# Attention scores of a 512-token hybrid block: one float32 product with half-zero keys per head, or two fp32r products of stacked query parts

## Chip, cores and metric

The kernel runs on one core of a Trainium2 chip. The metric is the device time of one execution in microseconds (us); less is better. The program is straight-line: five in-order instruction queues (TensorE, VectorE, ScalarE, GpSimd, and SyncE, which issues the DMAs), tied by semaphores.

## What is computed

Two transformer-like blocks run one after the other on 512 tokens of width 1024. The change lies in the first block's sliding-window attention. It has 16 query heads and 4 key/value heads of 64 features, 16 "meta" tokens that every query sees, and a window of 128 tokens:

```python
q = (q * (HEAD_DIM ** -0.5)).reshape(b, l, N_KV_HEADS, Q_PER_KV, HEAD_DIM)
...
keys = jnp.concatenate([k_meta, kn], axis=1)       # 16 meta + 2 blocks of 128
sc = jnp.einsum('bqkgd,bskd->bkgqs', qn, keys).astype(jnp.float32)
mask = jnp.concatenate([meta_ok, valid], axis=1)
p = sink_softmax(sc, mask, sink)
return jnp.einsum('bkgqs,bskd->bqkgd', p.astype(vals.dtype), vals)
```

The queries, keys and values come from `hn @ w_in`, where `hn` is a normalised state: each token's row carries a factor `r`, its reciprocal root mean square. Beside the attention the block has a state-space part (`s5_ssm`) and gates, all from the same `w_in`. Feed-forward layers and the second block make up the rest of the run.

## The kernel before

**Projections.** All big products are made of fp32r matmuls on split operands: a weight tile `raw` is fetched by DMA, ScalarE copies it to `whi` (fp32r), VectorE writes the rest `raw - whi` to `wlo` (`sub`, line 66), and `mm3` (line 182) adds three products hi*hi, lo*hi, hi*lo for each of eight slices of 128. A projection of 512 columns is 24 matmuls into one PSUM bank. `nat` (line 198) does the same for the values with 256 columns.

**The attention stage** (about 420 to 640 us of the run). After the state-space inputs `u` come two key projections. Each result is multiplied by `R` (the factor `r` spread over the columns) into `kf` and copied by ScalarE and GpSimd into window tiles `kw`: for each of two key heads a tile of 128 partitions whose other 64 partitions hold zeros, with three windows of 272 columns (16 meta columns and two blocks). Then the value projection, and four of eight query projections; `query` multiplies each by 0.125 and `R` on VectorE (line 83). One query tile holds two heads, one per 64 partitions.

Then a loop over eight units (two key pairs `pp` times four token blocks `n`). Unit `ui` issues:

- `scores1`: for each of four query tiles and both key heads `s_` one float32 product of 128 queries with W keys (144 columns for `n` = 0, "short", else 272, "long"; line 734). The zeros of `kw` take out the head that isn't meant. VectorE reads each product from PSUM in one instruction that adds the mask and finds the row maximum (line 737, called the reduction below), and later adds the sink terms; ScalarE takes the exponentials.
- in units 0, 1, 3 and 5 `ssm_quarter`: tiles `U`, `M`, `G`, `bstl`, `tab` come by DMA into single buffers; products with `bstl` (line 576) in two halves; VectorE multiplies and adds into `sq` tiles; two scans (lines 586, 587); more `sq` products; then per quarter 12 products (lines 597 to 599), a gelu, and a write to DRAM. The next quarter's `U` and `M` can be fetched only when the last of these 12 is done.
- in units 0 to 3 one more `query`; later three gate projections, which serve as work for TensorE.
- `turn1` and `values1` of the unit before: transposes (lines 766, 776) and products with the values (788, 792).

PSUM has two banks for projections and the state-space part (`b`), three for scores (`q`), two for transposes (`t`), one for the output (`o`).

**Order.** The recording layer schedules instructions within a queue, so that TensorE's and VectorE's queues interleave units, quarters and projections. Each queue then runs strictly in its order: an instruction that waits holds all behind it.

Of the kernel before, what the change touches and what calls it, by code (L numbers as in the profile page):

```python
# [53 lines left out]
def body(nc, tc, A, out, es):  # L54
# [13 lines left out]
    def mul(o, a, b, e=None):  # L68
        return tt(o, a, b, ALU.mult, e)
# [15 lines left out]
    def act(o, a, f, **kw):  # L85
        return SC.activation(o, a, f, **kw)  # L86
# [115 lines left out]
    def v2(t):  # L202
        return t.rearrange("p (a n) -> p a n", a=2)
# [453 lines left out]
    with tc.tile_pool(name="m1", bufs=1) as mp:  # L657
        att = mp.tile([P, 8, S], F32, name="att")
        with tc.tile_pool(name="m2", bufs=1) as ap_:
            kz = [[ap_.tile([P, 3, 272], F32, name=f"kw{mo}{e}") for e in range(2)] for mo in range(2)]  # L660
            for gs in kz:
                for e, g in enumerate(gs):
                    GP.memset(g[64 - 64 * e:128 - 64 * e], 0.0)
# [7 lines left out]
            kw = []  # L671
            for mo in range(2):
                p = proj(wload("w_in", 1024), P, 0, z, C528)
                f = ap_.tile([P, T1], F32, name="kf", tag=f"sq{mo}")
                mul(v2(f), p[:, :, :264], v2(R))

                gs = kz[mo]
                for e, g in enumerate(gs):
# [26 lines left out]
            qf = []  # L705

            def query():
# [5 lines left out]
            for _ in range(4):  # L713
                query()
# [8 lines left out]
            def scores1(u):  # L723
# [60 lines left out]
            def values1(u):  # L784
# [9 lines left out]
                act(att[:, pp * 4:pp * 4 + 4, n * P:(n + 1) * P], po.rearrange("p (i q) -> p i q", i=4), AF.Copy)  # L794

            units = [(pp, n) for pp in range(2) for n in range(4)]
            for ui in range(len(units) + 1):
# [4 lines left out]
                if ui < 4:  # L802
                    query()
                elif 5 <= ui < 8:
                    gate(zp.tile([P, aw], F32, name="acc" if ui == 5 else "sq", bufs=1 if ui == 5 else 2)[:, :S])
                elif ui == 8:
                    with tc.issue_after(last["sc"].ins):
                        for i in range(2):
                            gate(mp.tile([P, S], F32, name=f"q{i}"))
# [5 lines left out]
        with tc.tile_pool(name="m3", bufs=2) as gp_:  # L815
# [13 lines left out]
            for i in range(8):  # L829
# [3 lines left out]
                stt(ga, ga, 1.0, att[:, i], ALU.add, ALU.mult)  # L833
# [758 lines left out]
```

## Time and profile before

| | us |
|---|---|
| runs (3): lowest, median, highest | 2589.45, 2594.76, 2596.42 |
| profiled execution, whole | 2593.17 |
| its span, first to last instruction | 2591.3 |
| TensorE busy in the span | 2566.1 |
| VectorE busy in the span | 1573.6 |
| ScalarE busy in the span | 995.3 |

The profiled execution is 1.9 us longer than its span. A matmul's end is modelled in these profiles, so matmuls that follow each other are priced by the distance of their starts. A float32 matmul shows as two records.

### The profile page before, as it was taken

The page shows a single profiled execution, that of the slowest core. Times are in us where ns is not written, and L with a number is a line of the kernel's source. Part 1 is how long each engine was busy: PE and PEld are TensorE (multiplying, and loading weights), DVE is VectorE, ACT ScalarE, POOL GpSimd, SP SyncE. Part 2 cuts the span into 40 slices and gives each one's busy share as a digit, 9 for nine tenths or more (in the row PEclk, how much of TensorE's full clock was granted, in tenths as well). Part 3 has the DMA queues.
Part 4 walks back from the last instruction along what each step waited for, and adds up shares of the span by engine and source line. Part 5 has one row for each costly group of instructions (what it writes and reads, how often), then busy time and mean ns, then how long its engine had stood idle before and what let it go on. Part 6 is the DMA issues. An engine that isn't in the chain of part 4 may idle for free.

```text
span 2591.3 us, 35009 instructions
## 1 busy us (share of the span) xinstructions
PE 2566.1 (99%) x13918; PEld 2188.1 (84%) x13918; DVE 1573.6 (61%) x2859; ACT 995.3 (38%) x1562; POOL 84.9 (3%) x98
## 2 busy tenths in 40 slices
PE   9999999999999999999999999999999999999999
PEld 8999999766888888888888878888878888888887
DVE  7985445685467544467665775555763457655566
ACT  5222223445343222245544454333353234433333
POOL 0000001000000000000000001000000010100000
PEclk9999999999999999999999999999999999999999
DMA  5443324332333333322111223333232222333331
GB/s 182 132 136 113 92 90 133 104 94 68 100 97 101 98 98 96 95 90 70 53 58 62 76 78 108 98 98 98 82 100 58 75 65 83 120 98 98 98 96 67
DMA packets 87749, 243.32 MB, mean 94 GB/s; under 512 B 20081, under 2 KB 26097, under 8 KB 87458
## 3 DMA queue, kind: packets, MB, share of 16 engines
q1 hardware_dynamic: 87586, 241.08, 30.2%
q8 instruction: 110, 1.80, 0.3%
q14 instruction: 53, 0.43, 0.1%
HBM read 229.11 MB, written 11.93 MB: 93 GB/s over the span
## 4 chain that ended last, share of the span: by engine, by line
PE 96%; DVE 2%; issue 0%; SPq 0%; ACT 0%; DMA 0%; DVEq 0%
PE ps_b L182 27%; PE ps_q L182 19%; PE ps_t L182 18%; PE mm L182 16%; PE ps_b L198 5%; PE ps_o L1258 1%; PE ps_q L1230 1%; PE ps_o L792 1%; PE ps_q L734 1%; PE ps_t L1246 1%; PE ps_q L1384 1%; DVE sq L66 1%; PE ps_b L1457 0%; PE ps_t L198 0%; PE ps_t L776 0%
## 5 line engine op out<-in xcount | busy, mean ns | idle before, releaser
L86 ACT ACTIVATE whi<-raw 128x1024 fp32r<-128x1024 f32 (+2 forms) x418 | 432.8, 1038 | 1001.3 <-PE ps_b L182 297.5
L66 DVE TENSOR_TENSOR wlo<-raw,whi 128x1024 fp32r<-128x1024 f32 (+2 forms) x418 | 502.0, 1203 | 331.5 <-ACT whi L86 329.6
L182 PE MATMUL ps_b<-zh,whi 128*128 128x512 f32 (+1 forms) x692 | 272.8, 394 | 2.9 <-DVE sq L66 0.9
L182 PE MATMUL ps_b<-zl,whi 128*128 128x512 f32 (+1 forms) x692 | 269.8, 390 | 0.0
L182 PE MATMUL ps_b<-zh,wlo 128*128 128x512 f32 (+1 forms) x692 | 269.6, 390 | 0.0
L182 PE MATMUL ps_q<-zh,whi 128*128 128x512 f32 (+1 forms) x488 | 189.3, 388 | 1.2 <-ACT zh L86 1.2
L182 PE MATMUL ps_q<-zl,whi 128*128 128x512 f32 (+1 forms) x488 | 189.4, 388 | 0.0
L182 PE MATMUL ps_q<-zh,wlo 128*128 128x512 f32 (+1 forms) x488 | 189.2, 388 | 0.0
L182 PE MATMUL ps_t<-zh,whi 128*128 128x512 f32 x476 | 185.6, 390 | 0.6 <-ACT zh L86 0.6
L182 PE MATMUL ps_t<-zl,whi 128*128 128x512 f32 x476 | 185.6, 390 | 0.0
L182 PE MATMUL ps_t<-zh,wlo 128*128 128x512 f32 x476 | 185.2, 389 | 0.0
L182 PE MATMUL mm<-zh,whi 128*128 128x264 f32 x800 | 162.4, 284 | 5.8 <-ACT whi L86 5.8
L182 PE MATMUL mm<-zl,whi 128*128 128x264 f32 x800 | 161.8, 284 | 0.1
L182 PE MATMUL mm<-zh,wlo 128*128 128x264 f32 x800 | 161.3, 283 | 0.0
L182 PEld LDWEIGHTS ps_b<-zh,whi 128*128 128x128 f32 (+1 forms) x692 | 129.2, 187 | 33.6 <-issue 2.8
L182 PEld LDWEIGHTS ps_b<-zl,whi 128*128 128x128 f32 (+1 forms) x692 | 129.3, 187 | 28.8 <-issue 2.3
L182 PEld LDWEIGHTS ps_b<-zh,wlo 128*128 128x128 f32 (+1 forms) x692 | 129.2, 187 | 28.5 <-issue 1.1
L182 PEld LDWEIGHTS mm<-zh,whi 128*128 128x128 f32 x800 | 124.2, 189 | 5.8 <-ACT whi L86 5.8
L182 PEld LDWEIGHTS mm<-zl,whi 128*128 128x128 f32 x800 | 124.0, 189 | 0.4 <-DVE zl L83 0.4
L182 PEld LDWEIGHTS mm<-zh,wlo 128*128 128x128 f32 x800 | 123.9, 189 | 0.0
L182 PEld LDWEIGHTS ps_q<-zh,whi 128*128 128x128 f32 x488 | 91.6, 188 | 20.8 <-ACT zh L86 2.1
L182 PEld LDWEIGHTS ps_q<-zl,whi 128*128 128x128 f32 x488 | 91.6, 188 | 20.4 <-DVE zl L66 1.3
(586 smaller groups left out, 5340.2 us busy)
## 6 DMA issues: line engine op xcount, KB each, us to landing
raw<-in_ffn_w_dram SPq DMA_DIRECT2D x130, 512.0 KB, 3.5
raw<-in_w_up_dram SPq DMA_DIRECT2D x88, 512.0 KB, 3.7
raw<-in_w_down_dram SPq DMA_DIRECT2D x44, 512.0 KB, 3.6
raw<-in_w_in_dram SPq DMA_DIRECT2D x32, 512.0 KB, 3.6
raw<-in_mla_o_dram SPq DMA_DIRECT2D x16, 512.0 KB, 3.6
raw<-in_ple_g_dram SPq DMA_DIRECT2D x16, 512.0 KB, 3.7
raw<-in_glu_dram SPq DMA_DIRECT2D x8, 512.0 KB, 3.6
raw<-in_w_out_dram SPq DMA_DIRECT2D x8, 512.0 KB, 3.4
```

The lines of the kernel that those rows point to most:

```text
L66: return (e or V).tensor_tensor(o, a, b, op=op)
L86: return SC.activation(o, a, f, **kw)
L182: last["pe"] = PE.matmul(o[:, i, :c1 - c0], lhs, x[k][r][:, c0:c1], start=(k == 0 and j == 0), stop=(k == kt - 1 and j == 2))
L198: PE.matmul(o[:m, :n], x[k][a][:, t0:t0 + m], w[b][:, kk_ * c + m0:kk_ * c + m0 + n], start=(k == 0 and i == 0), stop=(k == kt - 1 and i = ...
L734: last["sc"] = PE.matmul(pq[s_][:, :W], qf[pp * 4 + i][:, n * P:(n + 1) * P], kw[pp][s_][:, max(n - 1, 0), :W])
L792: PE.matmul(po[64 * s_:64 * s_ + 64], vb[n - 1 + j][:, kv * 64:kv * 64 + 64], pT[s_][:, j], start=False, stop=(j == 1))
L1230: PE.matmul(p[:, :N], d["q"][e][:, bs], d["k"][e][:, :N], start=False, stop=True)
L1246: PE.transpose(pt[:, kt * P:(kt + 1) * P], sc[:, kt * P:(kt + 1) * P], ident)
L1258: PE.matmul(po[:, b * P:(b + 1) * P], vt[:, kt, e * P:(e + 1) * P], pT[:, kt * P:(kt + 1) * P], start=(kt == 0), stop=(kt == b))
L1384: PE.matmul(pu[c][:, :256], ek[b][rows, hc], vt[hh][rows, b])
```

## The change

For each unit the four query tiles are split once: ScalarE copies 64 partitions of all four (`x`, 64x512) to one half of a tile `qs` in fp32r, and VectorE writes the rest `x - copy` to the other half. The keys are split likewise (`keys`): `kh` holds the fp32r copy of the keys twice, on both halves of the partitions, and `kl` their rest twice. One product of `qs` with `kh` and one with `kl`, added in PSUM, then stand for the float32 product. The short windows are computed 256 columns wide, and read 144 wide.

The factor `r` of the queries is now applied by the reduction, which takes it as a value per partition (`r[:, n:n + 1]` instead of 1.0). So `query` is a plain scaled copy, on ScalarE. `keys(0)` follows the key projections; `keys(1)` is made in unit 3 into the same buffers. The second `kf` lies in the tile `acc`. The result `att` is two tiles, and the last two gates share a tile `gt`; both take over query buffers.

```diff
-            kz = [[ap_.tile([P, 3, 272], F32, name=f"kw{mo}{e}") for e in range(2)] for mo in range(2)]
...
-                f = ap_.tile([P, T1], F32, name="kf", tag=f"sq{mo}")
+                f = zp.tile([P, aw], F32, name="acc") if mo else ap_.tile([P, T1], F32, name="kf", tag="sq0")
                 mul(v2(f), p[:, :, :264], v2(R))
-
-                gs = kz[mo]
-                for e, g in enumerate(gs):
-                    r_ = slice(64 * e, 64 * e + 64)
-                    cpy = (lambda o, i: act(o, i, AF.Copy)) if e else GP.tensor_copy
-                    cpy(g[r_, 0], f[r_, :272])
-                    GP.tensor_copy(g[r_, 1:, 0:NM], f[r_, 0:NM].unsqueeze(1).to_broadcast([64, 2, NM]))
-                    for n in range(1, 3):
-                        cpy(g[r_, n, NM:], f[r_, NM + n * P:NM + (n + 2) * P])
-                kw.append(gs)
+                kf.append(f)
+
+            def keys(pp):
+
+                out_ = []
+                for e in range(2):
+                    a = slice(64 * e, 64 * e + 64)
+                    f = kf[pp][a]
+                    kh, kl = (ap_.tile([P, 3, 272], F32R, name=f"k{n}{e}") for n in "hl")
+                    for o in (a, slice(64 - 64 * e, 128 - 64 * e)):
+                        for w_, c in ((0, f[:, :272]), *((n, f[:, NM + n * P:NM + (n + 2) * P]) for n in (1, 2))):
+                            t = slice(NM if w_ else 0, 272)
+                            act(kh[o, w_, t], c, AF.Copy)
+                            sub(kl[o, w_, t], c, kh[a, w_, t].bitcast(F32))
+                        for k in (kh, kl):
+                            GP.tensor_copy(k[o, 1:, :NM], k[o, 0:1, :NM].to_broadcast([64, 2, NM]))
+                    out_.append((kh, kl))
+                return out_
+
+            kw = {0: keys(0)}
...
                 p = proj(wload("w_in", 1024), P, 0, z, C512)
-                t = (mp if len(qf) < 2 else ap_).tile([P, S], F32, name=f"q{len(qf)}")
-                stt(t, p[:, 0, :], 0.125, Rr, ALU.mult, ALU.mult)
-                qf.append(t)
...
+                act(qf[i // 4][:, i % 4], p[:, 0], AF.Copy, scale=0.125)
...
+                qs = []
+                for s_ in range(2):
+                    t = ap_.tile([P, 4, P], F32R, name=f"qs{s_}", bufs=2)
+                    a, o = slice(64 * s_, 64 * s_ + 64), slice(64 - 64 * s_, 128 - 64 * s_)
+                    x = qf[pp][a, :, n * P:(n + 1) * P]
+                    act(t[a], x, AF.Copy)
+                    sub(t[o], x, t[a].bitcast(F32))
+                    qs.append(t)
                 for i in range(4):
                     pq = [pss("q"), pss("q")]
                     for s_ in range(2):
-                        last["sc"] = PE.matmul(pq[s_][:, :W], qf[pp * 4 + i][:, n * P:(n + 1) * P],
-                                               kw[pp][s_][:, max(n - 1, 0), :W])
+                        for k in range(2):
+                            last["sc"] = PE.matmul(pq[s_][:, :max(W, 256)], qs[s_][:, i],
+                                                   kw[pp][s_][k][:, max(n - 1, 0), :max(W, 256)],
+                                                   start=(k == 0), stop=(k == 1))
                     for s_ in range(2):
-                        V.tensor_tensor_reduce(sc[s_][:, i, :W], pq[s_][:, :W], mk, 1.0, -3.0e38,
+                        V.tensor_tensor_reduce(sc[s_][:, i, :W], pq[s_][:, :W], mk, r[:, n:n + 1], -3.0e38,
                                                ALU.add, ALU.max, st[s_][0][:, i:i + 1])
...
+                    query(4 + ui)
+                if ui == 3:
+                    kw[1] = keys(1)
```

Three places of the new order matter below. The first is VectorE's queue from the fourth query to the first reductions. Before (`q_5392` is the fourth query, `sq_...` quarter 0's products, `ISA sc,at` a reduction):

```order
L83 SCALAR_TENSOR_TENSOR q_5392<-ps_b,R 128x512
L737 ISA sc,at_5398<-ps_q,mask 128x144
L737 ISA at_5398 128x1
L737 ISA sc,at_5401<-ps_q,mask 128x144
L737 ISA at_5401 128x1
L737 ISA sc,at_5398<-ps_q,mask 128x144
L737 ISA at_5398 128x1
L66 TENSOR_TENSOR wlo<-raw,whi 128x1024
```

Now:

```order
L66 TENSOR_TENSOR sq_5507<-ps_b,tab 128x264
L66 TENSOR_TENSOR sq_5510<-ps_b,tab 128x264
L66 TENSOR_TENSOR wlo<-raw,whi 128x1024
L66 TENSOR_TENSOR sq_5508<-ps_b,tab 128x264
L66 TENSOR_TENSOR qs_5414<-q_5274,qs_5414 64x512
L66 TENSOR_TENSOR sq_5509<-ps_b,tab 128x264
L66 TENSOR_TENSOR sq_5507<-ps_b,tab 128x264
L66 TENSOR_TENSOR sq_5510<-ps_b,tab 128x264
L66 TENSOR_TENSOR qs_5417<-q_5274,qs_5417 64x512
L66 TENSOR_TENSOR qs_5611<-q_5274,qs_5611 64x512
L66 TENSOR_TENSOR qs_5614<-q_5274,qs_5614 64x512
L752 ISA sc,at_5408<-ps_q,mask,rs_y 128x144
```

The first reduction, which opened the unit, now stands behind four query subtractions (units 0 and 1) and seven products of the quarter. The two products of the second half that free the last `b` bank stand right behind it.

The second is VectorE's queue in quarter 2, between its two halves. Before, the fourth product of the first half (`sq_6014`) and the first two of the second:

```order
L66 TENSOR_TENSOR sq_6014<-ps_b,tab 128x264
L737 ISA sc,at_6150<-ps_q,mask 128x144
L737 ISA at_6150 128x1
L66 TENSOR_TENSOR sq_6011<-ps_b,tab 128x264
L66 TENSOR_TENSOR sq_6014<-ps_b,tab 128x264
```

Now (`kl_6169`, `kl_6187` are the rests of the second pair's keys):

```order
L66 TENSOR_TENSOR sq_6077<-ps_b,tab 128x264
L752 ISA sc,at_5975<-ps_q,mask,rs_y 128x272
L752 ISA at_5975 128x1
L66 TENSOR_TENSOR kl_6169<-acc,kh_6168 64x272 x2
L66 TENSOR_TENSOR kl_6169<-acc,kh_6168 64x256 x4
L752 ISA sc,at_5978<-ps_q,mask,rs_y 128x272
L752 ISA at_5978 128x1
L66 TENSOR_TENSOR at_5975<-at_5975,sink 128x4
L793 COPY pT<-ps_t 128x512
L66 TENSOR_TENSOR kl_6187<-acc,kh_6186 64x272 x2
L66 TENSOR_TENSOR kl_6187<-acc,kh_6186 64x256 x4
L66 TENSOR_TENSOR sq_6074<-ps_b,tab 128x264
```

All twelve key subtractions have come between the halves (`x4` stands for two windows of two halves).

The third is TensorE's queue at the end of quarter 1. Before, its first closing product (line 598) stood between the rows of the seventh projection:

```order
L598 MATMUL ps_b<-sq_5667,G 128x128
L182 MATMUL ps_b<-zh_4665,wlo 128x512
L182 MATMUL ps_b<-zh_4669,whi 128x512
L182 MATMUL ps_b<-zl_4670,whi 128x512
L182 MATMUL ps_b<-zh_4669,wlo 128x512
L776 MATMUL ps_t<-ident,sc 128x128 x4
L792 MATMUL ps_o<-pT,vb_5179 64x512
L792 MATMUL ps_o<-pT,vb_5206 64x512
L599 MATMUL ps_b<-sq_5669,G 128x128
```

Now it stands ahead of that projection, with three of unit 3's pairs before it:

```order
L807 MATMUL ps_o<-pT,vb_5191 64x512
L748 MATMUL ps_q<-kh_5083,qs_5981 128x272
L748 MATMUL ps_q<-kl_5084,qs_5981 128x272
L748 MATMUL ps_q<-kh_5101,qs_5984 128x272
L748 MATMUL ps_q<-kl_5102,qs_5984 128x272
L748 MATMUL ps_q<-kh_5083,qs_5981 128x272
L748 MATMUL ps_q<-kl_5084,qs_5981 128x272
L598 MATMUL ps_b<-sq_5704,G 128x128
L599 MATMUL ps_b<-sq_5706,G 128x128
```

## Rows read from the trace of the kernel before

**Rows 1.** Page, busy time of each engine over the span, share, instructions.
```profile
PE 2566.1 (99%) x13918; PEld 2188.1 (84%) x13918; DVE 1573.6 (61%) x2859; ACT 995.3 (38%) x1562; POOL 84.9 (3%) x98
```
**Rows 2.** Windows between the four quarters' first scans: length, busy per engine, clock.
```profile
477.89:485.92 8.03, 6.84 (x45) 5.92 (x44) 8.03 (x33) 2.11 (x2) 0.00 (x0) 1.00 0.41 131
485.92:515.74 29.82, 24.55 (x129) 18.45 (x128) 26.22 (x91) 19.29 (x70) 1.17 (x3) 1.00 0.36 102
515.74:548.39 32.65, 31.74 (x159) 21.54 (x158) 25.04 (x73) 14.34 (x36) 0.84 (x2) 1.00 0.35 96
548.39:574.69 26.30, 25.86 (x134) 17.71 (x133) 22.18 (x71) 13.76 (x45) 1.15 (x3) 1.00 0.40 111
574.69:632.00 57.31, 57.05 (x260) 38.57 (x259) 35.34 (x93) 30.02 (x78) 0.62 (x2) 1.00 0.17 51
```
**Rows 3.** Chain that ended last, TensorE pieces: start, length, what, records.
```profile
419.32 17.30 PE mm L182 x143
...
581.72 1.38 PE ps_q L734 x6
...
592.37 0.87 PE ps_t L776 x8
593.25 1.05 PE ps_o L788 x2
594.30 1.00 PE ps_o L792 x2
```
**Rows 4.** Timeline of the second block's first fp32r score pair on TensorE.
```profile
1209.13 0.28 PE L1228 MATMUL ps_q<-kh,qr 128*128 128x256 f32 x1
1209.24 0.28 PE L1229 MATMUL ps_q<-kl,qr 128*128 128x256 f32 x1
```
**Rows 5.** Groups on VectorE by form.
```profile
L83 DVE SCALAR_TENSOR_TENSOR zl<-h,vec,zh 128x528 fp32r<-128x528 f32 x16 | 12.1, 764 | 6.7 <-ACT zh L86 6.7
L66 DVE TENSOR_TENSOR sq<-sq,tab 128x528 f32<-128x528 f32 x16 | 11.0, 698 | 0.1
...
L66 DVE TENSOR_TENSOR sq<-ps_b,tab 128x264 f32<-128x264 f32 x32 | 12.4, 426 | 3.3 <-PE ps_b L576 2.7 <-DMA y_d<-y 0.3
...
L586 DVE TENSOR_TENSOR_SCAN sq<-tab,sq 128x528 f32<-128x528 f32 x4 | 5.0, 1250 | 0.0
```
**Rows 6.** Timeline of VectorE: runs of equal instructions, start and length of the run.
```profile
479.18 1.22 DVE L66 TENSOR_TENSOR wlo<-raw,whi 128x1024 fp32r<-128x1024 f32 x1
480.31 1.45 DVE L66 TENSOR_TENSOR sq<-ps_b,tab 128x264 f32<-128x264 f32 x4
...
553.42 1.32 DVE L66 TENSOR_TENSOR sq<-sq,sq 128x528 f32<-128x528 f32 x2
```
**Rows 7.** Groups on ScalarE by form.
```profile
L86 ACT ACTIVATE pTm<-ps_t 64x512 f32<-64x512 f32 x8 | 4.6, 581 | 3.4 <-PE ps_t L766 3.4
...
L86 ACT ACTIVATE kw<-kf 64x256 f32<-64x256 f32 x4 | 1.4, 398 | 0.0
```
**Rows 8.** Timeline at the second key projection and the values.
```profile
435.90 1.40 DVE L66 TENSOR_TENSOR wlo<-raw,whi 128x1024 fp32r<-128x1024 f32 x1
440.81 0.71 DVE L66 TENSOR_TENSOR kf<-mm,R 128x528 f32<-128x528 f32 x1 [3.50 <-PE mm L182]
...
441.66 0.27 PE L198 MATMUL ps_b<-whi,zh 128*16 128x256 f32 x1 [0.89 <-ACT whi L86]
```
**Rows 9.** Timeline at the start of unit 0.
```profile
477.66 1.06 ACT L86 ACTIVATE whi<-raw 128x1024 fp32r<-128x1024 f32 x1 [4.33 <-PE ps_b L182]
...
483.94 0.47 PE L182 MATMUL ps_b<-zh,whi 128*128 128x512 f32 x1 [0.18 <-DVE sq L66]
```
**Rows 10.** Chain that ended last: marks A, B and C of the prediction.
```profile
513.53 5.72 PE ps_b L182 x24
...
557.07 0.22 PE ps_b L599 x2
...
576.24 5.49 PE ps_b L182 x24
```

More of the change, by code (lines that the diff above doesn't have):

```diff
@@ L657, in body @@
     with tc.tile_pool(name="m1", bufs=1) as mp:
-        att = mp.tile([P, 8, S], F32, name="att")
+        att = [mp.tile([P, 4, S], F32, name="att0")]
         with tc.tile_pool(name="m2", bufs=1) as ap_:
-            kz = [[ap_.tile([P, 3, 272], F32, name=f"kw{mo}{e}") for e in range(2)] for mo in range(2)]
-            for gs in kz:
-                for e, g in enumerate(gs):
-                    GP.memset(g[64 - 64 * e:128 - 64 * e], 0.0)
             for i4 in range(4):
@@ L670, in body @@
                 nc.sync.dma_start(u_d[i4 * P:(i4 + 1) * P], uf.rearrange("p j m -> p (j m)"))
-            kw = []
+            kf = []
             for mo in range(2):
                 p = proj(wload("w_in", 1024), P, 0, z, C528)
-                f = ap_.tile([P, T1], F32, name="kf", tag=f"sq{mo}")
+                f = zp.tile([P, aw], F32, name="acc") if mo else ap_.tile([P, T1], F32, name="kf", tag="sq0")
                 mul(v2(f), p[:, :, :264], v2(R))
-                gs = kz[mo]
-                for e, g in enumerate(gs):
-                    r_ = slice(64 * e, 64 * e + 64)
-                    cpy = (lambda o, i: act(o, i, AF.Copy)) if e else GP.tensor_copy
-                    cpy(g[r_, 0], f[r_, :272])
-                    GP.tensor_copy(g[r_, 1:, 0:NM], f[r_, 0:NM].unsqueeze(1).to_broadcast([64, 2, NM]))
-                    for n in range(1, 3):
-                        cpy(g[r_, n, NM:], f[r_, NM + n * P:NM + (n + 2) * P])
-                kw.append(gs)
+                kf.append(f)
[15 more added lines that the diff above has]
+            kw = {0: keys(0)}
             banks(b=2, q=3, t=2, o=1)
@@ L704, in body, with query @@
                     vb.append(t)
-            qf = []
-            def query():
+            qf = [mp.tile([P, 4, S], F32, name=f"q{i}") for i in range(2)]
+            def query(i):
                 p = proj(wload("w_in", 1024), P, 0, z, C512)
-                t = (mp if len(qf) < 2 else ap_).tile([P, S], F32, name=f"q{len(qf)}")
-                stt(t, p[:, 0, :], 0.125, Rr, ALU.mult, ALU.mult)
-                qf.append(t)
-            for _ in range(4):
-                query()
+                act(qf[i // 4][:, i % 4], p[:, 0], AF.Copy, scale=0.125)
+            for i in range(4):
+                query(i)
             live = {}
@@ L793, in values1 @@
                                   start=False, stop=(j == 1))
-                act(att[:, pp * 4:pp * 4 + 4, n * P:(n + 1) * P], po.rearrange("p (i q) -> p i q", i=4), AF.Copy)
+                act(att[pp][:, :, n * P:(n + 1) * P], po.rearrange("p (i q) -> p i q", i=4), AF.Copy)
             units = [(pp, n) for pp in range(2) for n in range(4)]
@@ L802, in body @@
                 if ui < 4:
-                    query()
+                    query(4 + ui)
+                if ui == 3:
+                    kw[1] = keys(1)
+                if ui == 4:
+                    att.append(mp.tile([P, 4, S], F32, name="att1", tag="q0"))
                 elif 5 <= ui < 8:
@@ L806, in body @@
                 elif ui == 8:
+                    gt = mp.tile([P, 4, S], F32, name="gt", tag="q1")
                     with tc.issue_after(last["sc"].ins):
                         for i in range(2):
-                            gate(mp.tile([P, S], F32, name=f"q{i}"))
+                            gate(gt[:, i])
                 if ui >= 1:
@@ L832, in body @@
                 ga, gs = gate_tiles[2 * i:2 * i + 2]
-                stt(ga, ga, 1.0, att[:, i], ALU.add, ALU.mult)
+                stt(ga, ga, 1.0, att[i // 4][:, i % 4], ALU.add, ALU.mult)
                 wg = wload("glu", 1024)
```

## Prediction

> **What bounds the kernel now.** I read the page first: TensorE is busy over 99% of the span [rows 1]. So work taken from TensorE is time gained wherever it never waits. Next, the windows over the attention stage, cut at the first scan of each quarter. There the picture is mixed. In the first two windows VectorE is busy 8.03 of 8.03 us and 26.22 of 29.82, TensorE 6.84 and 24.55: VectorE sets the pace. In the third and fourth TensorE has 31.74 of 32.65 and 25.86 of 26.30, but VectorE is at 25.04 and 22.18, with 11.7 us left in both together. In the last TensorE is full and VectorE has 22 us free [rows 2]. ScalarE is busy about 80 of the 154 us, so its new copies have room. The stage is thus where TensorE is relieved and VectorE is loaded, and what counts is which of them ends last in each window.
>
> **What TensorE saves.** Six units of eight products are long (48), two are short (16), and each product shows as two records. Six long records take 1.38 us, so 0.23 each and 0.46 for a long product [rows 3]; a short one is 144/272 of that, 0.24. An fp32r matmul of 264 columns takes 17.30/143 = 0.121 us [rows 3]; I take 0.125 for 272. For 256 columns the starts of a pair are 0.11 apart [rows 4]; I take 0.12. Now: 96 at 0.125 and 32 at 0.12 make 15.8 us against 48 x 0.46 + 16 x 0.24 = 25.9. TensorE saves 10.1 us, all in long units: 0.21 per product.
>
> **What VectorE gets.** Equal instructions follow each other at (1.45 - 0.426)/3 = 0.34 us for 264 columns and 1.32 - 0.70 = 0.62 for 528 [rows 5, 6]. Whether 64 partitions are cheaper than 128 no row on VectorE tells; on ScalarE 64x512 takes 581 ns [rows 7] where half of the 1.06 of a full-height 1024 columns [rows 9] would be 530. So I count the full price (bounds: half, 8.9 us, and all, 17.7). So 16 query subtractions cost 0.60 (9.6 us) and 24 key subtractions 0.34 (8.1). The reduction now takes a value per partition. No row shows this reduction with one; another instruction, with such a value, takes 764 ns where plain ones of its size take 698 [rows 5], so I add 0.066 to each of 64 (4.2 us; bounds 0 and 4.2). Eight query multiplications leave (0.62 each, 5.0 us). Net +16.9 us, or +12.7 without the surcharge on the reductions.
>
> [...]
>
> **ScalarE and GpSimd.** ScalarE gets 16 copies at 0.58, eight query copies at about the same, and 24 key copies for six, at 0.40 [rows 7]: some 21 us, beside 74 us of free time. It matters only where a copy is first in a chain. GpSimd's 16 small copies serve windows 1 and 2, first used two units later. They cost nothing as long as those two units cover them; VectorE's weight rest took 1.40 instead of 1.22 us beside such a copy [rows 6, 8], so if each of the 16 met one, 2.9 us.
>
> **Where the loads fall: three places.** *Keys.* VectorE does 12 subtractions (4.1 us) ahead of the second key multiplication. It is free from 437.3, the end of a weight rest, so it is done at 441.4 and the multiplication at 442.1 instead of 441.5; the values began at 441.66 [rows 8]. Cost 0.4 us, or nothing if the new PSUM tiles need not wait for that bank.
>
> *Unit 0.* The fourth query's projection ends at 477.7; ScalarE then first splits a weight, until 478.7 [rows 9], copies the query (479.3), and makes the query parts (the first by 479.9). VectorE's first reduction now stands behind a weight rest (480.31 - 479.18 = 1.13 [rows 6]), seven half-size products (7 x 0.34) and four query subtractions (4 x 0.60). That is 5.9 us from 478.7, when four products of line 576 (0.23 each) have followed the projection: 484.6. Reduction and two more products (1.0) free the bank for the next projection: 485.6 for 483.94, +1.7 us [rows 9]. With the 0.4 of the keys quarter 0 ends 2.1 us later. U and M are single-buffered, so quarter 1 starts later by that; VectorE's rows between the first two scans add up to the same in both orders (27.3 and 27.1 us without the reductions' surcharge). So the next projection, **mark A** (513.53 [rows 10]), comes at 515.6.
>
> *Quarter 2 and unit 4.* `keys(1)` writes the buffers of `keys(0)`, so it waits for unit 3's last pair, and its subtractions stand between quarter 2's halves. Added up by kind, VectorE's rows grow from 25.6 to 28.6 us between scans 2 and 3 and from 22.8 to 25.7 between 3 and 4; the surcharge on some 26 reductions adds 1.7. Some falls into the 11.7 us of free time. In the new order quarter 1's closing products stand ahead of a projection, so quarter 2 can begin sooner: from mark A a projection (5.4), transposes and value products (2.9) and VectorE's rest of quarter 1 (two scans, eight operations at 0.62, some reductions: 9.8) bring its end to 527.7. Then TensorE does the seventh projection, three value products and the rest of unit 3, and reaches its last pair near 540. From there VectorE has, in its order, 12 key subtractions (4.1), four products of the second half (1.4), eight operations at 0.62 and two scans at 1.17 (7.3; a scan's 1.25 [rows 5] less the overlap), a normalisation of 1024 columns and some 25 small ones (4.2): 557. The 12 closing products follow, 0.22 each with a wait between the first two: 559.6 for 557.3 (**mark B** [rows 10]).
>
> For unit 4 VectorE then has a weight rest, a gelu and four query subtractions (1.13 + 1.1 + 2.4) ahead of the first reduction, 562, and up to **mark C**, the first gate projection after scan 4, some 11.6 us of reductions, products and copies. TensorE's pairs follow them through three banks, so 575.6 for 576.2 [rows 10].
>
> **The ledger.** At each mark I take the delay and the difference in TensorE work still to come.
> - A: +2.1 us. Before, 8 short and 29 long products are left (15.3 us); now 8 short pairs and 32 long (9.9). Balance -3.3.
> - B: +2.3. Left before 2 short and 24 long (11.5), now 8 and 24 (7.9), but 8 more transposes at 0.11 [rows 3]. Balance -0.4.
> - C: -0.6. Left before 12 long (5.5), now 17 (4.3), and a unit's 12 transposes and three value products (1.3 + 1.05 + 2.0 [rows 3]) that were done before. Balance +2.5; with the surcharge of the reductions up to C, +4.5.
>
> Behind C TensorE is the bound in both. So the walk ends 2.5 to 4.5 us later. It puts every wait behind the other; what the schedule hides of the last two places shortens it, down to A's balance. I take about the middle of -3.3 and +4.5: **+1 us**. The 2593.17 of the profiled execution become 2594.2; that execution lies 1.6 below the median of the runs, so on their scale 2596. A difference under 0.3% (7.8 us) cannot be told from none here.
>
> **The rivals.** *TensorE stays the bound everywhere* (0.14). For it: the stage's TensorE is busy 146 of 154 us and VectorE has 37 us free in sum. Against it: 22 of these lie behind scan 4, where nobody waits for it, and the first 38 us are VectorE's. It gives the full 10.1: 2583 on the profile's scale, 2585 on the runs'. With only the 2.1 of the first two places lost it is 8.0, at the edge of what can be told.
>
> *VectorE's chain decides, and it is slower* (0.13). Place: between scans 2 and 4. If the 11.7 us of free time there are waits that stay (for score products, and for U and M), the 5.9 us and the surcharge of 1.7 come on top: scan 4 (576.7 in the walk, +2.0) is 9.7 later, mark C at +7.1, balance +10.2, so 2605. It decides as soon as mark C comes later than 580.9 (balance +7.8). For it: the reductions waited for score products, which now come at VectorE's pace; and `keys(1)` can't start early. Against it: quarter 2 may start sooner.
>
> *The pair is no cheaper than the float32 product* (0.03, slower). Then nothing is saved, and 2 to 16 us are lost (the first two places alone, or VectorE's net 16.9 but for what its 22 us behind scan 4 take); the pair in the second block speaks against it [rows 4].
>
> The forecast, a balance within 7.8 us, has 0.70. That makes 0.14 faster, 0.70 the same, 0.16 slower. For the range I go out on both sides until about 0.08 each is left: 2585, the first rival's full gain, and 2604, short of the second's price. The likeliest case alone spans 2587 to 2602.
>
> **What would show it.** TensorE's score group should come to about 16 us by starts, at 0.25 per long pair; if it is 0.4, the first term is wrong. The first reduction should stand near 485, the following projection near 486 and mark A near 515.6: if these keep their old times, the delay of unit 0 was hidden by work that I queued too strictly. VectorE's busy time over the span should rise by 12 to 20 us (1573.6 before [rows 1]), each reduction taking some 0.07 us longer. Between scans 3 and 4 TensorE should wait several microseconds where it waited 0.44 [rows 2], for `qs` and `sq`. If instead the waits are no longer than before and the run ends 8 us or more early, the ledger at B and C was wrong, and VectorE had the room after all.

## Result, and the profile after

The changed kernel took 2614.3 us (median of 6 runs, 2606.59 to 2616.55) against 2594.8 for the kernel before: ratio 1.0074, 95% interval 1.0060 to 1.0087. It is 19.5 us slower, outside the forecast range. The profiled execution took 2616.11 us, its span 2614.1.

The page of the changed kernel, busy time by engine, answers to [rows 1]:

```profile
PE 2577.6 (99%) x13918; PEld 2194.3 (84%) x13918; DVE 1593.1 (61%) x2891; ACT 1015.4 (39%) x1604; POOL 82.8 (3%) x100
```

VectorE is 19.5 us busier, as far as foreseen. But TensorE, which was to lose 10 us of work, is 11.5 us *busier*, and idle for 36.5 us of the span instead of 25.2. The windows between the quarters' first scans say why; they are cut as in [rows 2] (length, busy of TensorE, its weight loads, VectorE, ScalarE and GpSimd, granted clock, DMA share, GB/s):

```profile
481.60:491.49 9.89, 6.39 (x32) 4.73 (x31) 9.18 (x24) 3.90 (x6) 0.00 (x0) 0.91 0.32 106
491.49:522.84 31.35, 26.05 (x110) 19.10 (x108) 27.50 (x90) 17.90 (x55) 0.83 (x2) 0.72 0.33 87
522.84:560.86 38.02, 34.92 (x177) 24.49 (x178) 29.05 (x81) 20.19 (x53) 3.60 (x11) 0.95 0.34 101
560.86:595.42 34.56, 30.56 (x129) 20.89 (x128) 26.58 (x77) 17.84 (x52) 0.84 (x2) 0.80 0.26 73
595.42:656.95 61.53, 59.29 (x280) 39.16 (x278) 41.38 (x113) 36.67 (x98) 0.93 (x3) 1.00 0.17 48
```

The five windows last 175.35 us for 154.11 before. TensorE is idle in 18.14 of them for 8.07 (+10.1) and busy in 157.21 for 146.04 (+11.2). The score products, the only ones that changed, take 24.2 us of it instead of 28.0 (each record from its start to the next one's, and at most its own length). So the rest, which is the same work, took some 15 us more. The clock column shows why: 0.91, 0.72, 0.95 and 0.80, where before it was 1.00 in all five. Length times missing clock, summed over the windows, is 18.5 us. That is the most that the clock can have cost here, because idle time is in it too.

The chain that ended last shows the two levels side by side (start, length, tile, line, records):

```profile
516.85 0.85 PE ps_t L791 x4
517.70 2.00 PE ps_o L803 x2
519.70 1.18 PE ps_b L576 x4
520.88 1.90 PE ps_o L807 x2
...
526.46 5.50 PE ps_b L182 x24
531.96 0.87 PE ps_t L791 x8
532.83 1.05 PE ps_o L803 x2
533.88 1.00 PE ps_o L807 x2
```

The value products take 2.00 and 1.90 us at 517.70 and 520.88, and 1.05 and 1.00 for the same shapes at 532.83 and 533.88; in [rows 3] they took 1.05 and 1.00. Four transposes take 0.85, eight 0.87. The granted clock was 0.50 from 516.85 to 519.70 and from 520.88 to 522.78, and 1.00 from 531.96 to 534.90.

The falls came behind waits and thin work. The first lies in the values: TensorE had waited 2.5 us for VectorE, and from 445.2 on the starts are 0.21 apart instead of 0.12 (granted clock 0.83 between 440 and 450 us). The longest lasts from 506.8 to 523.8 (granted clock 0.50): from 502.2 on TensorE had had five score pairs to do, between waits of 0.2, 0.9 and 0.2 us for the reductions, and then 1.0 for the transfer of `M`. TensorE's five largest waits between 435 and 660 us, by what ended them (total, times, longest):

```profile
PE ps_q L748 <- DVE at L752: 4.4, 7, 1.1
PE ps_q L748 <- DVE qs L66: 3.4, 3, 2.2
PE ps_b L198 <- DVE acc L66: 2.5, 1, 2.5
PE ps_b L576 <- DVE at L766: 2.3, 1, 2.3
PE ps_b L576 <- DVE sq L66: 1.7, 2, 1.0
```

All five are for VectorE; the next are 1.7 us for the transfer of a weight tile, 1.2 for VectorE and 1.0 for that of `M`. The values (line 198) wait for the multiplication into `acc`, which stands behind the key subtractions; the score products (748) wait for the new query parts and for the longer reductions.

The cost of VectorE's new work, in groups by form (busy, mean ns of one; [rows 5] had none of these):

```profile
L752 DVE CUSTOM_DVE_ANT_0 sc<-ps_q,mask,rs_y 128x272 f32<-128x272 f32 x48 | 22.5, 495 | 6.5 <-PE ps_q L748 6.4
L66 DVE TENSOR_TENSOR qs<-q,qs 64x512 fp32r<-64x512 f32 x16 | 11.0, 686 | 0.5
L752 DVE CUSTOM_DVE_ANT_0 sc<-ps_q,mask,rs_y 128x144 f32<-128x144 f32 x16 | 5.3, 364 | 1.9 <-PE ps_q L748 1.8
L66 DVE TENSOR_TENSOR kl<-kf,kh 64x256 fp32r<-64x256 f32 x8 | 3.4, 420 | 0.1
L66 DVE TENSOR_TENSOR kl<-kf,kh 64x272 fp32r<-64x272 f32 x4 | 1.8, 440 | 0.1
```

And its timeline at the keys and at unit 0, where [rows 8, 9] stood (start, length of the run):

```profile
437.59 5.35 DVE L66 TENSOR_TENSOR kl<-kf,kh 64x272 fp32r<-64x272 f32 x12
442.98 0.71 DVE L66 TENSOR_TENSOR acc<-mm,R 128x528 f32<-128x528 f32 x1
```

```profile
486.25 2.12 DVE L66 TENSOR_TENSOR qs<-q,qs 64x512 fp32r<-64x512 f32 x3
488.41 0.37 DVE L752 CUSTOM_DVE_ANT_0 sc<-ps_q,mask,rs_y 128x144 f32<-128x144 f32 x1
```

Twelve key subtractions in 5.35 us follow each other at 0.45, three query subtractions at 0.71: each takes its full length, and nothing of it lies under its neighbour. The pair itself is what was forecast. TensorE's timeline, where [rows 4] showed the second block's:

```profile
497.73 0.29 PE L748 MATMUL ps_q<-kh,qs 128*128 128x272 f32 x1
497.85 0.29 PE L748 MATMUL ps_q<-kl,qs 128*128 128x272 f32 x1
```

The starts are 0.12 apart, so a pair costs about 0.25 where pairs follow each other. Behind another instruction or a wait the first product takes longer, 0.20 here behind two products of line 598:

```profile
498.39 0.36 PE L748 MATMUL ps_q<-kh,qs 128*128 128x272 f32 x1
498.59 0.29 PE L748 MATMUL ps_q<-kl,qs 128*128 128x272 f32 x1
```

**Clock and time from run to run.** One number needs the single runs: the granted clock differs between executions of one and the same program. The six runs of the changed kernel go from 2606.59 us at a mean clock of 0.994 to 2616.55 at 0.989, 2.0 us per 0.001. The kernel before, in 75 runs taken beside the experiments, goes from a median of 2587.2 at 0.998 (8 runs) to 2596.3 at 0.994 (4 runs), 2.3 per 0.001. At the one clock that both kernels had, 0.994, the changed one is 10 us slower (2606.59, a single run, against 2596.3). By that, about half of its loss stands beside the clock, and half goes with it.

### The profile page after: what moved, and what is told of

It is laid out like the page before. It is cut to its first block, busy times and chain, and to the rows that moved or that the text cites. A ratio compares the mean times of both kernels' runs of the same rounds, so it can differ in the third digit from the quotient of the medians.

```text
span 2614.1 us, 35099 instructions
## 1 busy us (share of the span) xinstructions
PE 2577.6 (99%) x13918; PEld 2194.3 (84%) x13918; DVE 1593.1 (61%) x2891; ACT 1015.4 (39%) x1604; POOL 82.8 (3%) x100
## 4 chain that ended last, share of the span: by engine, by line
PE 95%; DVE 3%; ACT 1%; DMA 1%; issue 0%; SPq 0%; POOL 0%; DVEq 0%; ACTq 0%
PE ps_b L182 26%; PE ps_q L182 19%; PE ps_t L182 18%; PE mm L182 16%; PE ps_b L198 5%; PE ps_o L1278 1%; PE ps_q L1250 1%; PE ps_t L1266 1%; DVE sq L66 1%; PE ps_q L1404 1%; PE ps_o L807 1%; PE ps_t L198 0%; PE ps_b L1477 0%; PE ps_q L1248 0%; PE ps_q L1249 0%
```

## Experiments

The theory after this reading: VectorE's longer chain makes TensorE wait; the cheaper products leave it nothing to do meanwhile; its clock falls (0.50 in the stretch above), and it then does its own work at that clock. The rivals: the waits alone; the pointer in the reduction; the transfers between the quarters. All ratios are to the kernel before, with 95% intervals. The recording layer orders each version anew, so every edit also moves some instructions in the queues; differences of a few us between versions carry that with them.

### TensorE's load against VectorE's load

**e1_float32** undoes the product alone:

```diff
-                        for k in range(2):
-                            last["sc"] = PE.matmul(pq[s_][:, :max(W, 256)], qs[s_][:, i],
-                                                   kw[pp][s_][k][:, max(n - 1, 0), :max(W, 256)],
-                                                   start=(k == 0), stop=(k == 1))
+                        last["sc"] = PE.matmul(pq[s_][:, :W], qs[s_][:, i].bitcast(F32),
+                                               kw[pp][s_][0][:, max(n - 1, 0), :W].bitcast(F32))
```

> The changed kernel with its pair of products put back to one float32 product of the same operands (the low part of the keys is still made, but no product reads it, so scores have the high keys alone). VectorE's, ScalarE's and GpSimd's work is that of the changed kernel; TensorE gets its 10.1 us back (48 products at 0.46 in place of pairs at 0.25). Theory 1, the clock: waits for VectorE alone cost some 10 us, and the rest of the loss is TensorE at half clock after them, because the shorter products leave it idle. Then the granted clock of the attention stage stays near 1.00, mean 0.994 or more, and the time is 2600 to 2612, not above the changed kernel in spite of the work added. Rival, waits only: the half clock lies under the waits and costs nothing; the added work goes on top of TensorE's busy stretches, and the time is 2616 to 2625.

Measured: 2607.62 us, 1.0045 [1.0024, 1.0066], clock 0.994 in the profile. More work on TensorE, and no more time than the changed kernel (1.0074; the intervals just overlap): as theory 1 has it. Two things qualify it. No product reads `kl` here, so a wait for `kl` can't hold TensorE either; **e7_pairs_twice** below has no such gap. And two of its five runs had a clock of 0.997 and 0.998 and still took 2601.3 and 2601.2 us, 12 to 14 us more than the kernel before at those clocks: this part is waits without the clock.

**e2_no_subs** takes the 40 subtractions away:

```diff
-                            sub(kl[o, w_, t], c, kh[a, w_, t].bitcast(F32))
-                    out_.append((kh, kl))
+                    out_.append((kh, kh))
...
-                    sub(t[o], x, t[a].bitcast(F32))
```

> The changed kernel without its 16 query and 24 key subtractions: the low half of the stacked query is zero, set once, and the second product reads the high keys again, so the low parts are left out of the scores. TensorE has the same instructions as the changed kernel. Theory 1, VectorE's added chain: with some 21 us of subtractions gone (16 at 0.69, 24 at 0.42) the first values start back at 441.7, the first reductions near 484, and no long wait is left for the clock to fall in: mean clock 0.995 or more, time 2583 to 2596. Rival, the shorter products by themselves leave TensorE short of work and its clock falls whatever VectorE does: mean clock 0.992 or less and a time of 2600 to 2612.

Measured: 2597.95 us, 1.0014 [1.0004, 1.0023], clock 0.993. The subtractions are worth 16 us with the pairs. That is their load on VectorE and the products' wait for them together, which this version doesn't separate. Neither expectation was right in full: the time missed theory 1's 2596 by 2, and the clock missed 0.995. Its waits name the next cause, the transfers of the next quarter:

```profile
PE ps_b L576 <- DMA M<-k_d: 5.4, 2, 3.3
PE ps_q L750 <- DVE at L754: 1.4, 3, 0.9
PE ps_b L576 <- DVE sq L66: 1.3, 2, 1.0
```

**e6_float32_no_subs** joins both edits.

> The fourth corner beside the changed kernel (pairs, with subtractions), e1_float32 (float32 products, with them) and e2_no_subs (pairs, without): one float32 product of the same operands and no subtractions, so low parts are left out of the scores here too. TensorE's and VectorE's work is then near that of the kernel before, but for the longer reductions and the queries that ScalarE makes. Theory 1: the cheaper pairs cost time only when TensorE has waits to fall into, so without the subtractions they are worth their 10 us or some part of it, and this kernel is slower than e2_no_subs: 2598 to 2606. Rival, seen in e2_no_subs, whose clock still fell (0.51 in 500 to 510, 0.66 in 540 to 550) while TensorE waited for the next quarter's transfer: the pairs are worth nothing even there, TensorE gets to the transfer earlier and waits; then this kernel has a clock of 0.995 or more and a time of 2590 to 2598, not slower than e2_no_subs.

Measured: 2595.90 us, 1.0016 [1.0004, 1.0027], clock 0.997. The rival was right: without the subtractions the pair is worth nothing (1.0014 against 1.0016). With them it costs 0.3% (1.0074 against 1.0045). So the product that was to save 10 us shows up as a gain in neither.

**e7_pairs_twice** adds work instead of replacing it:

```diff
-                        for k in range(2):
+                        for k in (0, 1, 0, 1):
```

> The changed kernel with each pair of products issued twice into the same bank, the second time over the first: 64 more pairs at 0.25, 16 us of work on TensorE that the result doesn't need. All other engines do what they did. Theory, the clock: as in e1_float32, the work fills waits in which the clock fell; mean granted clock 0.993 or more and a time of 2600 to 2616, not above the changed kernel by more than 2. Rival, e1_float32 was faster through its form or its order of instructions and not through a busier TensorE: the 16 us come on top, 2622 to 2632.

Measured: 2609.23 us, 1.0061 [1.0045, 1.0077], clock 0.995. TensorE has 64 pairs more to do, 16 us (0.6%) at 0.25 and 12.7 by their starts (36.9 for 24.2), and the kernel is not slower than the changed one. Its page:

```profile
PE 2576.3 (99%) x14046; PEld 2200.8 (84%) x14046; DVE 1593.4 (61%) x2891; ACT 1016.2 (39%) x1604; POOL 83.1 (3%) x100
```

TensorE's busy time is 1.3 us *below* the changed kernel's 2577.6, with 128 instructions more. The windows of both, for 490 to 540 and 540 to 590 us, the changed kernel first:

```profile
490.00:540.00 50.00, 44.70 (x202) 32.57 (x202) 42.25 (x130) 28.24 (x84) 1.68 (x4) 0.80 0.28 79
540.00:590.00 50.00, 43.76 (x202) 29.67 (x200) 36.99 (x98) 24.63 (x61) 3.59 (x11) 0.86 0.36 103
```

```profile
490.00:540.00 50.00, 46.70 (x279) 37.66 (x277) 45.16 (x134) 30.20 (x87) 1.68 (x4) 1.00 0.33 95
540.00:590.00 50.00, 44.91 (x248) 32.43 (x247) 43.36 (x128) 28.08 (x78) 3.90 (x11) 0.97 0.30 88
```

In the same 100 us TensorE gets 527 instructions through instead of 404, at clocks of 1.00 and 0.97 instead of 0.80 and 0.86. Of the 527, 184 are score products, and half of these are repeats; without them it is still ahead, with 435. The added work came for nothing while the clock stayed up. That the one made the other is the reading that fits, but the order of the queues changed as well.

### The pieces of VectorE's load

**e4_scale_exp**:

```diff
-                                               mk, r[:, n:n + 1], -3.0e38,
+                                               mk, 1.0, -3.0e38,
...
-                    tt(mx, mx, sk, ALU.max)
+                    stt(mx, mx, r[:, n:n + 1], sk, ALU.mult, ALU.max)
...
-                        act(t[:, i, :W], t[:, i, :W], AF.Exp, bias=nb[:, i:i + 1], accum_out=dn[:, i:i + 1])
+                        act(t[:, i, :W], t[:, i, :W], AF.Exp, scale=r[:, n:n + 1], bias=nb[:, i:i + 1], accum_out=dn[:, i:i + 1])
```

> The changed kernel with the reduction's scale back at the constant 1.0; the token's factor is applied to the maximum (one instruction in place of the one that was there) and as the scale of the exponential. Nothing is left out. Theory 1, the pointer of the 64 reductions (495 against 435 ns, 364 against 300) is 4 us of VectorE's chain and so part of the loss: the reductions go back to 435 and 300 ns, the time falls by 2 to 6 us to 2608 to 2612. Rival, the 4 us lie beside other waits: reductions shorter, time within 2 us of the changed kernel.

Measured: 2607.50 us, 1.0046 [1.0031, 1.0061], 7 us less than the changed kernel. The reduction is back where it was:

```profile
L752 DVE CUSTOM_DVE_ANT_0 sc<-ps_q,mask 128x272 f32<-128x272 f32 x48 | 19.6, 435 | 5.0 <-PE ps_q L748 4.8
```

Forty-eight at 60 ns and sixteen at 64 are 3.9 us of VectorE (its page has VectorE 2.0 us less busy, 1591.1). The time fell by more than that; how much of it is the order of the queues is not shown.

**e5_gp_subs** gives every `sub` of the change to GpSimd (`sub(..., GP)`).

> The changed kernel with its 40 subtractions on GpSimd in place of VectorE. Nothing is left out. No trace so far shows a subtraction on GpSimd; its memsets ran 128x512 in 0.53 us and its fp32r copies 64x32 in 0.20 to 0.30. Theory 1, VectorE's chain is the cause: VectorE is 21 us lighter, and if a subtraction takes GpSimd 1 us or less, the time is 2588 to 2600; if it takes 1.5 us or more, 12 of them in a row before the values and before unit 4 cost more than VectorE's did, and the time stays above 2605. Rival, VectorE's load is not the cause: 2610 to 2620 at any price.

Measured: 2605.55 us, 1.0043 [1.0028, 1.0058]: theory 1's second case, at its edge (1.49 us for a query subtraction, 0.7 to 1.1 for a key one). GpSimd was slow, and parts of VectorE's work slower beside it; GpSimd's query group and VectorE's first scans in this run:

```profile
L66 POOL TENSOR_TENSOR qs<-q,qs 64x512 fp32r<-64x512 f32 x16 | 23.8, 1489 | 50.5 <-ACT qs L86 49.8
...
L586 DVE TENSOR_TENSOR_SCAN sq<-tab,sq 128x528 f32<-128x528 f32 x4 | 6.1, 1523 | 0.0
```

A query subtraction took 1.49 us instead of 0.69, and the scan 1523 ns on average where [rows 5] has 1250: two of the four, which began while GpSimd subtracted, took 1.77 and 1.83 us, the other two 1.25. Not all of it slows: a scan of line 587 beside the same subtractions, at 557.02, took its usual 1.24. (GpSimd was busy for 6.23 of the 10 us from 480, for 9.46 of those from 550, and for 0.31 of those from 520, where a first scan took 1.25.) VectorE's busy time fell by 10.0 us (1593.1 to 1583.1), not by the 21.3 that left it.

**c2_fewer_subs** makes each low part of the keys once:

```diff
-                            sub(kl[o, w_, t], c, kh[a, w_, t].bitcast(F32))
...
+                    sub(f[:, :272], f[:, :272], kh[a, 0].bitcast(F32))
+                    sub(f[:, 272:T1], f[:, 272:T1], kh[a, 2, NM:].bitcast(F32))
+                    for o in rows:
+                        for w_, c in wins:
+                            act(kl[o, w_, NM if w_ else 0:], f[:, c], AF.Copy)
...
             for i in range(4):
                 query(i)
+                if i == 1:
+                    kw[0] = keys(0)
```

> A version that takes VectorE's share of the loss apart from the result: the changed kernel with 8 key subtractions in place of 24 (each low part made once, in place, and copied to its windows and its other half by ScalarE, 24 copies of some 0.43), with the first keys made behind the second query and not ahead of the values, and with the scale in the exponential as in e4_scale_exp. Nothing is left out. VectorE is lighter by 6.7 + 4 us. Theory 1 (VectorE's chain, then the clock): values start at 441.7 again, unit 4 is not behind 12 subtractions, time 2592 to 2602. Rival, the query subtractions inside the units (16 at 0.69) are what holds TensorE: still 2603 to 2608, as e4_scale_exp.

Measured: 2602.48 us, 1.0039 [1.0026, 1.0053]. Just above theory 1's range, and 12 us below the changed kernel. **c4_fewer_subs_gp** sends its query subtractions to GpSimd.

> c2_fewer_subs with its 16 query subtractions on GpSimd, where they took 1.49 each in e5_gp_subs. Nothing is left out. VectorE is lighter by another 11 us, less what it loses while GpSimd works (two scans took 1.8 us in place of 1.25 in e5_gp_subs). Theory 1: 2588 to 2598, 3 to 8 below c2_fewer_subs. Rival, GpSimd's slower subtraction (0.8 longer before each unit's first score) and VectorE's slowed work give it back: within 3 us of c2_fewer_subs or above.

Measured: 2607.39 us, 1.0056 [1.0036, 1.0076]: the rival. **c5_before_scale** is a side step: it lightens VectorE in the kernel before.

> The kernel before, float32 products over zeros as they were, with only the queries' factor moved: ScalarE makes the eight queries (as in the changed kernel) and the token's factor is the scale of the exponential, with no added instruction on VectorE, which loses 8 at 0.62, 5 us. Nothing is left out. Theory 1, VectorE's chain in this stage sets TensorE's waits of the kernel before (9.4 us of idle between 440 and 640): faster by 1 to 5 us, 2587 to 2592 against 2592. Rival, those waits are for the next quarter's transfers: no difference, within 1 us.

Measured: 2599.42 us, 1.0022 [1.0011, 1.0032]. Slower, against both expectations, with VectorE 3.1 us less busy (1570.5 for 1573.6). Its granted clock is 0.54 between 510 and 520 us, behind waits of up to 3.4 us (for `y` of VectorE) that the kernel before has not. I didn't find out whether the queries on ScalarE or the new order of the queues made them. The changed kernel contains the same move of the queries, so up to 7 us of its loss may be this.

### The transfers between the quarters

The next quarter's U products wait for a DMA that waits for the last product on the old `U`. **u1_after_two_u**, **u2_before_two_u** and **u3_no_subs_two_u** put the `U` of quarters 0 and 2 in another buffer:

```diff
-        U = sp.tile([P, 4, MC], F32, name="U")
+        U = zp.tile([P, aw], F32, name="sq", bufs=2)[:, :4 * MC].rearrange("p (a m) -> p a m", a=4) \
+            if q % 2 == 0 else sp.tile([P, 4, MC], F32, name="U")
```

> The changed kernel with the tile U of quarters 0 and 2 in another buffer, so that a quarter's transfer of U doesn't wait for the last product of the quarter before it. Nothing is left out, no engine gets or loses work. If the transfer between two quarters is what TensorE runs into, the time falls by 3 to 8 us to 2606 to 2611. If VectorE's chain is what it waits for in this kernel (11 of 20 us of waits are put down to it), the time stays within 3 us of 2614.

> The kernel before with the same second buffer for U. Its trace has 1.6 us of waits that are put down to the transfers of a quarter; by that the time falls by 1 to 4 us, 2588 to 2591. If the idle stretches are those of VectorE's chain: within 1 us of 2592.

> e2_no_subs (pairs, no subtractions, low parts left out) with the second buffer for U. e2_no_subs waited 5.4 us for the transfers, and its clock fell behind two of these waits. If these transfers are what swallows the 10 us that the pairs save, the saving now shows: 2584 to 2592. If TensorE is short of work in this stage whatever it waits for, the wait moves to another place and the time stays 2594 to 2599.

Measured: u1 2600.58 us, 1.0032 [1.0022, 1.0042]; u2 2591.09, 0.9993 [0.9983, 1.0003]; u3 2596.43, 1.0009 [0.9998, 1.0019].

u1 gained 14 us, more than either expectation. The transfer did come free: the first four U products of quarter 1 start at 496.54 instead of 506.79. But the next four wait for VectorE:

```profile
496.54 0.72 PE L577 MATMUL ps_b<-U,bstl 128*128 128x132 f32 x4 [0.32 <-ACT q L86]
508.52 1.22 PE L577 MATMUL ps_b<-U,bstl 128*128 128x132 f32 x4 [2.79 <-DVE y L83]
```

In sum TensorE's idle time stayed (35.8 us of the span for 36.5), and its busy time fell from 2577.6 to 2561.7. So the gain isn't less waiting. It goes with a higher granted clock, mean 0.993 for 0.989, and what in the new order brought that is not settled.

In u3 the transfer's wait is gone, and others stand in its place:

```profile
PE ps_t L784 <- DVE mt L66: 4.2, 2, 3.0
PE ps_t L794 <- ACT pTm L86: 3.8, 2, 3.3
PE ps_q L751 <- DVE at L755: 3.3, 4, 2.4
```

That left one question: is it these waits that eat the pair's gain, or the clock behind them? **f2_no_subs_two_u_twice** is u3 with each pair issued twice; **f1_fewer_subs_two_u** joins c2 and u1; **f3_fewer_subs_two_u_twice** is f1 with each pair twice.

> u3_no_subs_two_u (low parts left out) with each pair issued twice, 16 us more on TensorE. If the half clock is what costs u3_no_subs_two_u its gain, the clock is back at 0.996 or more and the time 2588 to 2597, not above u3_no_subs_two_u. If the saved work only becomes waits, at no loss by the clock, the added work fills them first and then adds: 2600 to 2612.

> c2_fewer_subs (8 key subtractions in place of 24, keys behind the second query, scale in the exponential) with the second buffer for U of u1_after_two_u. Nothing is left out. If the transfer's wait (13.7 us in u1_after_two_u against the changed kernel) and VectorE's part (11.8 in c2_fewer_subs) are separate costs, both together pass the kernel before: 2585 to 2594. If they are one and the same wait, seen from two sides, the time is that of the better one: 2596 to 2603.

> f1_fewer_subs_two_u with each pair issued twice. Nothing is left out. By the clock: clock 0.995 or more, time within 3 us of f1_fewer_subs_two_u or below it. By waits alone: 5 to 16 us above it.

Measured: f2 2593.98 us, 1.0008 [0.9998, 1.0017], clock 0.997; f1 2598.50, 1.0027 [1.0016, 1.0038], clock 0.994; f3 2606.78, 1.0059 [1.0042, 1.0075], clock 0.995.

f2 equals u3 with 64 pairs more work. The windows from 490 to 590 us, u3 first:

```profile
490.00:540.00 50.00, 42.87 (x219) 30.60 (x217) 37.71 (x125) 31.10 (x92) 2.54 (x7) 0.90 0.30 89
540.00:590.00 50.00, 45.07 (x218) 30.30 (x219) 40.16 (x123) 33.98 (x98) 1.56 (x5) 0.93 0.29 82
```

```profile
490.00:540.00 50.00, 47.82 (x278) 36.22 (x276) 40.01 (x128) 32.30 (x94) 2.25 (x7) 1.00 0.39 105
540.00:590.00 50.00, 48.55 (x281) 37.31 (x280) 42.59 (x122) 34.28 (x98) 2.54 (x6) 1.00 0.27 77
```

TensorE is idle for some 12 us of these 100 in u3, and length times missing clock is 8 to 9 more. Filled, both are used, and the end stands still: TensorE is not the bound of this stretch. f1 equals u1 within the intervals, so the two repairs do not add up. f3 is the miss: its clock is at the 0.995 that was expected, and still the second pair cost 8 of its 16 us, as its expectation has it for waits alone. So filling was free in two pairs of versions and not in the third.

No version beat the kernel before beyond its interval; u2, which leaves the products alone, is the only one below 1.

## Why the prediction was wrong

**The pair's price: right for pairs in a row, too low for the group.** Back to back it is 0.12 per product and 0.25 per pair, as forecast. But the sign asked for about 16 us by starts, and the whole group took 24.2, a little of it at a granted clock of 0.50: many first products come behind another instruction or a wait and take about 0.2. The float32 products took 28.0 by the same count, for the 25.9 of the forecast. So the saving is about 4 us in this trace, not 10.1, and none of it is seen in the time.

**VectorE's load: right in sum (+19.5 us busy, 12 to 20 forecast), wrong in one price.** The reductions grew by 60 and 64 ns for the 66 taken. The subtractions cost 21.3 us (11.0 for the queries, 10.3 for the keys), not 17.7. I had them overlap as in the run of four products of [rows 6]; on the chip they stand end to end: 686 ns for one of 512 elements and 0.71 us from start to start, 440 and 420 ns for 272 and 256 elements and 0.45 us from start to start.

**Keys: right in place, small in size.** The values began 2.2 us later (443.83), not 0.4, behind twelve subtractions at 0.45 each. And they ended 3.8 later, because TensorE's clock fell in them (0.89 over them, 1.00 over those of the kernel before). First the kernel before, then the changed one:

```profile
441.68 14.39 PE ps_b L198 x120
```

```profile
443.83 16.01 PE ps_b L198 x120
```

**Unit 0: right by itself.** The first reduction came at 488.41 for 484.6 and the next projection at 489.62 for 485.6. The 3.8 us that the reduction is late had come in with the values: from the end of ScalarE's weight split (482.50, forecast 478.7) to the first reduction it is the forecast 5.9. I had carried this through to mark A as a delay of 2.1 us; A came at 526.46, 12.9 late. Part of the projection, from 489.62 to 493.00, and then quarter 1's beginning, from 506.8 to 523.8, had a granted clock of 0.50.

**The ledger failed.** At each mark it set the delay against TensorE's work still to come, "the difference in TensorE work", at one price: the full clock that [rows 2] shows in every window. So a wait cost its own length, and less work behind it gave that length back. On the chip, waits and thinner work in the same stretch went with a lower clock (0.72 in the second window, 0.80 in the fourth), and TensorE paid for all its work there, not just for the scores. The balances of -3.3, -0.4 and +2.5 to +4.5 leave out the 18.5 us that the windows' clock column sums to. Mark B came at 570.78, 13.7 late (forecast +2.3), mark C at 603.10, 26.9 late (forecast -0.6); the end came 22.8 late. So the loss falls into two stretches that the walk had as nearly free: up to A, and from B to C, where unit 4's first reductions, its waits and the clock of 0.80 lie. The sign for scans 3 to 4 held: TensorE is idle there for 4.0 us instead of 0.44.

Two sums of the walk can't be followed from the terms beside them. From A at 515.6 the terms for quarter 1's end come to 533.7 one behind the other, and to 527.7 only if VectorE's 9.8 start 2.3 us after A, beside the projection. And 562 and 11.6 make 573.6, not the 575.6 given for mark C. The failure doesn't hang on either.

**The second rival named the engine and half of the price.** It put the loss between scans 2 and 4. Scan 4 came 20.7 late (595.42 for 574.69), 13.6 of it between these scans and 7.1 before them. Its +10.2 us is close to the 10 us that remain between the kernels at one clock, 0.994. That is partly luck: its mark C was to be 7.1 late and was 26.9. Its 2605 held no fall of the clock, and the range's upper end, 2604, stood on it.

What is shown: that the subtractions, with the waits for them, are the larger part of the loss (e2: 16 us); that beside them a TensorE with more to do finishes no later (e1, e7); and that the granted clock was higher in those runs (0.994 and 0.995, for 0.989). What stays open: the share of the order of the queues, which no version keeps fixed and which c5 suggests can be 7 us; why a second buffer for `U` gave back 14 us; and why f3 paid for its second pairs.

The change had a rival that I didn't write down: work taken from an engine that waits is not only worth nothing, it can cost. The pairs of windows above bear it out, 0.80 and 0.86 of the clock with the single pairs against 1.00 and 0.97 with the doubled ones.

## To carry over

Before taking work from TensorE, look stretch by stretch at who ends last there; where it is another engine, the saved work becomes a wait, and a wait may cost more than its length if the granted clock falls, as here to 0.72 and 0.80 in the second and the fourth window. Read the clock column of such a stretch as a price per instruction, and ask what the shorter work and the longer waits together do to it. When a split operand is the price of a cheaper product, count its preparation on the engine that already sets the pace, each instruction at its full length, unless a row of the same form shows overlap.

## What the runs showed of the hardware

- TensorE's mean clock of one and the same program varied between executions: 0.994 to 0.998 in the kernel before, 0.993 to 0.998 in e1_float32, 0.989 to 0.994 in the changed one. Time moved by 2.0 to 2.3 us per 0.001.
- In this stage 128 added products (16 us at 0.25 per pair) cost nothing in e7 and f2 and 8 us in f3.
- Subtractions of 64 rows to fp32r took 686 ns for 512 elements and 0.45 from start to start for 256 and 272; so half the partitions gave no discount here (698 ns for 528 elements on all of them [rows 5]).
- GpSimd took 1.49 us for a 64x512 subtraction to fp32r (VectorE 0.69). Two of VectorE's four first scans, those that began beside GpSimd's subtractions, took 1.77 and 1.83 us instead of 1.25.
- An fp32r product of 272 columns started 0.12 behind the one before it, and about 0.2 of time went by behind a first one that followed another form.
